# Three rearrangements of small TensorE work in a hybrid decoder layer: the adaLN columns, eight narrow transposes, and the bank of the state-space preparation

## The chip, the cores and the metric

The kernel runs on one core of a Trainium2 chip. The metric is the device time of one execution in microseconds.

## The reference

One decoder layer on 256 tokens of width 1024, all float32: a SwiGLU block (width 2816), then a mixing block (block-sparse attention with 8 heads beside a diagonal state-space layer with 32 groups, merged by sigmoid gates), then a second SwiGLU block, then a final norm. Each sub-layer's input is normalized, scaled and shifted, and its output is gated, by vectors that come from one conditioning vector c:

```python
ada = jax.nn.silu(c) @ w_ada[l] + b_ada[l]
sh1, sc1, g1, sh2, sc2, g2, sh3, sc3, g3 = jnp.split(ada, N_ADA, axis=-1)
h = modulate(rmsnorm(x, norm_ffn1[l]), sh1, sc1)
x = x + 0.5 * g1[:, None, :] * swiglu(h, w_ffn1_in[l], w_ffn1_out[l])
```

The nine vectors (numbers 0 to 8) have 1024 elements each. The kernel needs each as 128 partitions by 8 columns.

## The kernel before

Every weight comes from memory as float32, 1 MB at a time, into a ring of four buffers `raw`. ScalarE casts half of a buffer to `w_hi` (L296), VectorE makes the rest `w_lo` (L304), and each product is three matmuls (high by high, high by low, low by high): L327 to L329 for the tiles that go through `mm3`, L500 to L502 for the output projections, L649 for the first feed-forward's opening. One half buffer is a "quantum"; `state["q"]` counts them. A tile, or one step of an output projection, takes one quantum and is 24 matmuls with 256 columns.

Small TensorE work is put between the tiles by two means. `fill()` runs after most tiles and takes the first entry of the deque `pe_fill` if its due number has been reached. `pump()` moves the generator `ssm_prep` (the state-space preparation, 4 transposes of 128x128 at a time at L896, L910 and L935, and 64 small matmuls at L923) by one `yield`. A scheduler orders the traced instructions of every engine by what it takes to be ready, except inside `manual_schedule`; every engine then runs its list in that order, and a PSUM bank or a buffer that is taken anew waits for all readers and writers of its last use.

Vectors 0 and 1 are made at the start. The other seven are summed by VectorE over four weight blocks (`consume_ada`, L276) and handed to `ada_done`, which queues `do_cols` four quanta later. `do_cols` does all in one go, in one PSUM bank: eight passes with a matrix of ones add the partitions (L403), ScalarE copies the row sums to `ada_rows` (L408), two float32 products with four columns each (four passes, L410) turn them, and VectorE adds the bias (L390 to L395). The bank is `state["bank"]`: 3 in the first feed-forward and up to the four tiles that fill `U`, 1 in the 16 gate tiles and the branches behind them, 3 from the output projection on. The preparation uses banks 2 and 3.

The fills of the seven vectors, by the quantum at which they are due: vector 2 at 28, 4 at 42, 3 at 56 (first feed-forward), 5 at 84 (the last of the four `U` tiles), 7 at 92 and 6 at 100 (gate tiles; quanta 101 and 102 have no fill, 103 is the first branch tile), 8 at 162 (second feed-forward). `final_gain` (L1436) transposes the eight rows of `norm_final`, which a DMA puts in `rows[0]` (L1433), and is due at 148; the first fill of the second feed-forward is at 127. `rows[0]` held the vector c before that and was last read at the start (L1038).

Of the kernel before, what the change touches and what calls it, by code (L numbers as in the profile page):

```python
# [14 lines left out]
ALU = mybir.AluOpType  # L15
# [4 lines left out]
KD = D // 128  # L20
# [11 lines left out]
FILL_DELAY = 4  # L32
# [23 lines left out]
def kernel(ctx, tc, T, out):  # L56
    nc = tc.nc
# [33 lines left out]
    def bank(i):  # L91
        return psum.tile([128, 512], F32, tag=f"bank{i}", name=f"bank{i}")

    def sb(tag, shape, dt=F32, bufs=1, name=None):
        return parts[place.get(tag, "pool")].tile(shape, dt, tag=tag, name=name or tag, bufs=bufs)
# [129 lines left out]
    state = {"loaded": 0, "split": 0, "q": 0, "bank": 3}  # L225
# [4 lines left out]
    pe_fill = deque()  # L230
# [34 lines left out]
    def consume_ada(i):  # L265
        v, j = raw_items[i][3:]
        r = raw_tiles.pop(i)
        if j == 0:
            acc[v] = sb("acc", [128, D], bufs=2)
        a = acc[v]  # L270
        for k in range(2):
            cs = csil[:, 2 * j + k, 0:1]
            if j == 0 and k == 0:
                nc.vector.tensor_scalar(a, r[:, k, :], cs, None, op0=ALU.mult)
            else:
                nc.vector.scalar_tensor_tensor(out=a, in0=r[:, k, :], scalar=cs, in1=a, op0=ALU.mult, op1=ALU.add)  # L276
        if j == 3:
            ada_done(v)
# [53 lines left out]
    rows = [const.tile([n, 128], F32, name=f"rows{i}") for i, n in enumerate((8, 80, 56))]  # L332
# [23 lines left out]
    ident = const.tile([128, 128], F32, name="ident")  # L356
# [9 lines left out]
    bada = cols0[:, 0:72].rearrange("p (v k) -> p v k", k=KD)  # L366
    ldt = const.tile([128, 16], F32, name="ldt")
    norm_cols = {1: cols0[:, 72:80], 4: cols[:, 32:40], 7: cols[:, 40:48]}
# [15 lines left out]
    ada = {v: const.tile([128, KD], F32, name=f"ada{v}") for v in range(9)}  # L384

    def ada_cols(v, p, ks):

        o, b = ada[v][:, ks], bada[:, v, ks]
        if v in norm_cols:
            nc.vector.scalar_tensor_tensor(out=o, in0=p, scalar=1.0, in1=b, op0=ALU.add, op1=ALU.add)  # L390
            nc.vector.tensor_tensor(out=o, in0=o, in1=norm_cols[v][:, ks], op=ALU.mult)
        else:
            nc.vector.tensor_tensor(out=o, in0=p, in1=b, op=ALU.add)
            if v % 3 == 2:
                nc.vector.tensor_scalar(o, o, 0.5, None, op0=ALU.mult)  # L395

    def ada_done(v):
        a = acc.pop(v)

        def do_cols():  # L400
            p = bank(state["bank"])
            for q in range(4):
                nc.tensor.matmul(  # L403
                    p[32 * q:32 * q + 32, 0:256], ones[:, 0:32], a[:, q * 256:(q + 1) * 256], start=True, stop=True,
                    tile_position=(0, 32 * q),
                )
            rs = sb("ada_rows", [128, 256])
            nc.scalar.copy(rs, p[:, 0:256])  # L408
            for n in range(2):
                nc.tensor.matmul(  # L410
                    p[:, 256 + n:264:2], rs[:, n * 128:(n + 1) * 128], ident[:, ::32], start=True, stop=True
                )
            ada_cols(v, p[:, 256:264], slice(0, KD))

        pe_fill.append((state["q"] + FILL_DELAY, do_cols))

    block_sb = {}

# [14 lines left out]
    def ada_block_cols(b):  # L433
        a = block_sb.pop(b)
        p = bank(7)
        for n in range(2):
            nc.tensor.matmul(p[:, n:n + 1], a[:, n * 128:(n + 1) * 128], one1, start=True, stop=True)
        ks = slice(b, b + 1)
        ada_cols(1, p[:, 0:1], ks)
        ada_cols(0, p[:, 1:2], ks)  # L440
# [282 lines left out]
    def scratch(n):  # L723
        return [const.tile(P16, F32, name=f"scr{next(scr_n)}") for _ in range(n)]
# [107 lines left out]
    def ssm_prep():  # L832
# [10 lines left out]
        t, k, r, p = scratch(4)  # L843
# [45 lines left out]
        prep_ok[0] = False  # L889
        yield  # L890
        yield
        Cc = pcs[1]
        for i in range(2):
            p = bank(3)
            for j in range(4):
                nc.tensor.transpose(  # L896
                    p[:, j * 128:(j + 1) * 128], c_raw[i][:, j].rearrange("p a b -> p (a b)"), ident
                )
            pv = p.rearrange("p (i g c) -> p i g c", g=2, c=16)
            for g in range(2):  # L900
                rs = slice(64 * g, 64 * g + 64)
                for d in (Cc[i][rs], Cm[i][rs, :, g, :]):
                    nc.scalar.activation(d, pv[rs, :, g, :], AF.Copy, scale=-1.0 if i else 1.0)
            yield
        G = [sb(f"ssm_G{i}", [128, 16, 128]) for i in range(2)]
        for i in range(2):
            for q in range(4):
                p = bank(2 + q % 2)
                for n in range(4):
                    nc.tensor.transpose(  # L910
                        p[:, n * 128:(n + 1) * 128],
                        Gp[i][:, 4 * q + n].rearrange("p t g c -> p (t g c)"), ident,
                    )
                nc.scalar.copy(
                    G[i][:, 4 * q:4 * q + 4, :].rearrange("p a b -> p (a b)"), p
                )
                yield
        ssm["G"] = G
        p = bank(3)
        for j in range(4):  # L920
            for n in range(2):
                for q in range(4):
# [4 lines left out]
                        start=(n == 0), stop=(n == 1), tile_position=(0, 32 * q),  # L927
# [5 lines left out]
        p = bank(2)  # L933
# [10 lines left out]
        for t0 in range(4):  # L944
            rs = slice(32 * t0, 32 * t0 + 32)
# [81 lines left out]
    start = ExitStack()  # L1027
# [26 lines left out]
    for j in range(1, 4):  # L1054
# [19 lines left out]
        out=sel, in_=sel, compare_op=ALU.is_equal, fill=0.0, base=0, pattern=[[-1, 2], [0, 64]], channel_multiplier=1  # L1074
# [3 lines left out]
    for g in Gp + Cm + [ssm_L]:  # L1078
        nc.gpsimd.memset(g, 0.0)
    start.close()  # L1080
    prep = ssm_prep()

    def step1():
# [79 lines left out]
    for t in range(2):  # L1163
        nc.scalar.copy(vt[t], vb[t])

    U = sb("ssm_U", [128, 16, NC4 + 1])
    nc.gpsimd.memset(U[:, :, 0:1], 0.0)
    for j in range(4):
        p = bank(4 + j)[:, 0:S]
# [3 lines left out]
        for n in range(4):  # L1173
            for t in range(4):
                o = U[32 * t:32 * t + 32, 4 * j + n, 1:NC4 + 1]
                i_ = pv[32 * n:32 * n + 32, t, :]
# [7 lines left out]
    def s_mm(f):  # L1184
        S_b[f] = (bank(2), bank(3))
        for i in range(8):
            for n in range(2):
                nc.tensor.matmul(  # L1188
                    S_b[f][n][:, i * 64:(i + 1) * 64], ssm["G"][n][:, 8 * f + i, :],
                    U[:, 8 * f + i, 0:NC4], start=True, stop=True,  # L1190
                )
# [40 lines left out]
    def y_mm(f, m):  # L1232
# [5 lines left out]
        for y in range(3):  # L1238
            for n in range(4):
# [4 lines left out]
                else:  # L1244
                    st, mv = ssm["L"][:, ii, t, :], U[:, ii, 1:NC4 + 1]
                nc.tensor.matmul(  # L1246
# [96 lines left out]
    for hd in range(8):  # L1343
        n = 2 * hd - (hd > 6)
# [11 lines left out]
    for n in range(16):  # L1356
        g, j = divmod(n, 8)
        p = bank(4 + n % 3)[:, 0:S]
# [34 lines left out]
    for q in range(4):  # L1393
        p = bank(4 + q)
# [7 lines left out]
    for q in range(4):  # L1402
        p = bank(4 + q)
# [22 lines left out]
    ks = range(KD - HOLD, KD)  # L1426
# [11 lines left out]
        nc.tensor.transpose(p[:, 0:KD], rows[0], ident[0:8, 0:8])  # L1438
        nc.vector.tensor_copy(nf, p[:, 0:KD])

    pe_fill.append((state["q"] + 30, final_gain))

    def each(g):
        if g == 0:
# [37 lines left out]
    for t in range(2):  # L1482
        o = sb(("ssm_Pr", "ssm_Pi")[t], [128, D])
# [37 lines left out]
```

## Time and profile before

| | |
|---|---|
| median of 3 runs | 613.01 us (611.45 to 613.42) |
| the profiled execution | 611.65 us |
| its span, first to last instruction | 609.5 us |
| TensorE matmuls busy | 598.2 us (98%) x5328 |
| VectorE busy | 456.1 us (75%) |
| ScalarE busy | 326.9 us (54%) |
| mean granted TensorE clock | 0.988 |

A matmul's busy time is longer than the distance to the next one, since they are pipelined: 0.28 us each where a new one starts every 0.11 to 0.12 us. So the distance between starts is what to read, not the busy share. What lies outside the span is 2.1 us.

### The profile page before, as it was taken

Reading aid. Unit: us, or ns where it says so; the run is one execution under the profiler, and the core shown is the slowest. Engines: PE = TensorE matmul, PEld = TensorE weight load, DVE = VectorE, ACT = ScalarE, POOL = GpSimd, SP = SyncE. Lnnn points to the kernel's source line nnn. Section 1 sums busy time; section 2 is a strip of 40 time slices with the busy share of each in tenths; the row PEclk is TensorE's granted clock in tenths of the full one; section 3 lists DMA queues with packets and bytes.
Section 4 is the critical chain, followed back from the end, with each engine's and each line's share of the span. In section 5 each row is a group of like instructions: output and inputs, shape, how many; then the busy total and the mean of one; then the engine's idle time right before and its main releaser. Section 6 shows DMA issues by size and latency. Waiting matters only on the chain.

```text
span 609.5 us, 12820 instructions
## 1 busy us (share of the span) xinstructions
PE 598.2 (98%) x5328; PEld 571.3 (94%) x5328; DVE 456.1 (75%) x838; ACT 326.9 (54%) x537; POOL 25.3 (4%) x37
## 2 busy tenths in 40 slices
PE   7999999999999999999999999999999999999996
PEld 7888999999999999998987899999999999999995
DVE  2689999889867569998999859968975646445433
ACT  4445856469435445846536865447744444444434
POOL 6201010020000001000000000001000000000000
PEclk8999999999999999998999999999999999999997
DMA  9999989875969555888448836564586746745201
GB/s 278 335 312 247 362 276 368 280 263 177 317 212 343 178 172 172 312 270 284 139 140 282 276 135 208 195 221 139 208 275 209 247 168 233 249 149 200 70 2 70
DMA packets 97770, 136.70 MB, mean 224 GB/s; under 512 B 7761, under 2 KB 77474, under 8 KB 97712
## 3 DMA queue, kind: packets, MB, share of 16 engines
q1 hardware_dynamic: 97424, 135.81, 66.8%
q8 instruction: 42, 0.69, 0.5%
q14 instruction: 16, 0.13, 0.1%
q0 software_dynamic: 288, 0.07, 0.1%
HBM read 134.82 MB, written 1.05 MB: 223 GB/s over the span
## 4 chain that ended last, share of the span: by engine, by line
PE 88%; DVE 4%; DMA 4%; ACT 2%; issue 1%; POOL 0%; SPq 0%; ACTq 0%; DVEq 0%
PE bank L327 16%; PE bank L328 16%; PE bank L329 16%; PE bank L500 8%; PE bank L501 8%; PE bank L502 8%; PE bank L649 5%; DVE w_lo L304 2%; PE bank L425 1%; DMA raw<-in_w_in_dram 1%; PE bank L1246 1%; DMA raw<-in_w_ada_dram 1%; PE bank L1188 1%; DMA ssm_G<-in_w_ffn_in_dram 1%; DVE acc L276 1%
## 5 line engine op out<-in xcount | busy, mean ns | idle before, releaser
L304 DVE TENSOR_TENSOR w_lo<-raw,w_hi 128x1024 fp32r<-128x1024 f32 x168 | 204.2, 1223 | 84.2 <-ACT w_hi L296 83.8
L296 ACT CAST w_hi<-raw 128x1024 fp32r<-128x1024 f32 x168 | 174.0, 1048 | 165.5 <-PE bank L328 97.4
L327 PE MATMUL bank<-h_hi,w_hi 128*128 128x256 f32 x736 | 209.5, 285 | 0.0
L329 PE MATMUL bank<-h_hi,w_lo 128*128 128x256 f32 x736 | 207.1, 281 | 0.0
L328 PE MATMUL bank<-h_lo,w_hi 128*128 128x256 f32 x736 | 207.0, 281 | 0.0
L327 PEld LDWEIGHTS bank<-h_hi,w_hi 128*128 128x128 f32 x736 | 139.5, 190 | 3.9 <-issue 2.3
L329 PEld LDWEIGHTS bank<-h_hi,w_lo 128*128 128x128 f32 x736 | 140.0, 190 | 0.3 <-issue 0.2
L328 PEld LDWEIGHTS bank<-h_lo,w_hi 128*128 128x128 f32 x736 | 139.0, 189 | 0.1
L500 PE MATMUL bank<-a,w_hi 128*128 128x256 f32 x352 | 99.2, 282 | 0.0
L501 PE MATMUL bank<-a,w_hi 128*128 128x256 f32 x352 | 98.9, 281 | 0.0
L502 PE MATMUL bank<-a,w_lo 128*128 128x256 f32 x352 | 98.4, 280 | 0.0
L276 DVE SCALAR_TENSOR_TENSOR acc<-raw,csil,acc 128x1024 f32<-128x1024 f32 x49 | 62.8, 1281 | 7.8 <-DMA raw<-in_w_ada_dram 7.5
L500 PEld LDWEIGHTS bank<-a,w_hi 128*128 128x128 f32 x352 | 66.5, 189 | 1.0 <-issue 1.0
L502 PEld LDWEIGHTS bank<-a,w_lo 128*128 128x128 f32 x352 | 66.7, 190 | 0.0
L501 PEld LDWEIGHTS bank<-a,w_hi 128*128 128x128 f32 x352 | 66.1, 188 | 0.0
L327 PE MATMUL bank<-a,w_hi 128*128 128x258 f32 x112 | 31.9, 286 | 0.0
L328 PE MATMUL bank<-a,w_hi 128*128 128x258 f32 x112 | 31.8, 284 | 0.0
L329 PE MATMUL bank<-a,w_lo 128*128 128x258 f32 x112 | 31.5, 282 | 0.0
L649 PE MATMUL bank<-h_hi,w_hi 128*128 128x256 f32 x112 | 27.4, 294 | 0.9 <-ACT w_hi L296 0.5
L649 PE MATMUL bank<-h_lo,w_hi 128*128 128x256 f32 x112 | 27.8, 286 | 0.0
L649 PE MATMUL bank<-h_hi,w_lo 128*128 128x256 f32 x112 | 27.4, 283 | 0.0
L446 POOL TENSOR_TENSOR rstd<-rstd,mhalf 128x2 f32<-128x2 f32 x4 | 4.7, 1168 | 456.8 <-DVE rstd L445 456.8
(337 smaller groups left out, 893.0 us busy)
## 6 DMA issues: line engine op xcount, KB each, us to landing
raw<-in_w_ffn_in_dram SPq DMA_DIRECT2D x36, 1024.0 KB, 5.4
raw<-in_w_ada_dram SPq DMA_DIRECT2D x28, 1024.0 KB, 5.2
raw<-in_w_ffn_out_dram SPq DMA_DIRECT2D x22, 1024.0 KB, 5.3
raw<-in_w_in_dram SPq DMA_DIRECT2D x16, 1024.0 KB, 5.5
raw<-in_w_ada_dram SPq DMA_DIRECT2D x16, 512.0 KB, 8.1
raw<-in_w_out_dram SPq DMA_DIRECT2D x4, 1024.0 KB, 4.8
a<-in_w_ffn_in_dram SPq DMA_DIRECT2D x8, 448.0 KB, 7.1
ssm_G<-in_w_ffn_in_dram SPq DMA_DIRECT2D x4, 896.0 KB, 10.7
```

The source lines that it names most:

```text
L276: nc.vector.scalar_tensor_tensor(out=a, in0=r[:, k, :], scalar=cs, in1=a, op0=ALU.mult, op1=ALU.add)
L296: nc.scalar.copy(hi, r)
L304: nc.vector.tensor_tensor(out=lo, in0=r, in1=hi.bitcast(F32), op=ALU.subtract)
L327: nc.tensor.matmul(o, st[0], mv[0], start=first, stop=False)
L328: nc.tensor.matmul(o, st[0], mv[1], start=False, stop=False)
L329: nc.tensor.matmul(o, st[1], mv[0], start=False, stop=last)
L425: nc.tensor.matmul(p[q:q + 32, 0:256], csil[:, k, :], r[:, k, :], start=(k < 4), stop=(k >= 4), tile_position=(0, q))
L500: nc.tensor.matmul(mm3_o, wj[0], a[0], start=first and j % 2 == 0, stop=False)
L501: nc.tensor.matmul(mm3_o, wj[0], a[1], start=False, stop=False)
L502: nc.tensor.matmul(mm3_o, wj[1], a[0], start=False, stop=last and j % 2 == 1)
L649: nc.tensor.matmul(pb[b][:, n * S:(n + 1) * S], z[:, b * 128:(b + 1) * 128], h[hl][:, kb, :], start=(kb == 0 and n == 0 and y == 0), stop= ...
L1188: nc.tensor.matmul(S_b[f][n][:, i * 64:(i + 1) * 64], ssm["G"][n][:, 8 * f + i, :], U[:, 8 * f + i, 0:NC4], start=True, stop=True,)
```

## The change

`do_cols` becomes two entries of `pe_fill`. `sums` does the eight passes and the copy, and puts `turn_rows` at the head of the queue for the next quantum. `turn_rows` takes the bank anew, transposes the two halves of `ada_rows` whole (128x128, one pass each) and reads every 32nd column of the result; it then queues `spacer` for two quanta later. `spacer` takes the bank and transposes `rows[0]` (8 rows) into eight columns that nobody reads. One more `spacer` is queued ahead of the four `U` tiles. The preparation takes bank 2 for everything, and has one more `yield` before its first transposes. `final_gain` is due at 126 and no longer at 148.

```diff
     def ada_cols(v, p, ks):
-        o, b = ada[v][:, ks], bada[:, v, ks]
+        o, b, g = ada[v][:, ks], bada[:, v, ks], norm_cols[v][:, ks] if v in norm_cols else None
+        if len(p.shape) == 3:
+            o, b, g = (z if z is None else z.rearrange("p (q n) -> p q n", n=2) for z in (o, b, g))
...
+    def spacer():
+        p = bank(state["bank"])
+        nc.tensor.transpose(p[:, 0:8], rows[0], ident[0:8, 0:8])
+
     def ada_done(v):
         a = acc.pop(v)
-        def do_cols():
+        def sums():
             p = bank(state["bank"])
...
             rs = sb("ada_rows", [128, 256])
             nc.scalar.copy(rs, p[:, 0:256])
+            pe_fill.appendleft((state["q"] + 1, lambda: turn_rows(rs)))
+
+        def turn_rows(rs):
+            p = bank(state["bank"])
             for n in range(2):
-                nc.tensor.matmul(
-                    p[:, 256 + n:264:2], rs[:, n * 128:(n + 1) * 128], ident[:, ::32], start=True, stop=True
-                )
-            ada_cols(v, p[:, 256:264], slice(0, KD))
-        pe_fill.append((state["q"] + FILL_DELAY, do_cols))
+                nc.tensor.transpose(p[:, n * 128:n * 128 + 128], rs[:, n * 128:(n + 1) * 128], ident)
+            ada_cols(v, p[:, 0:256].rearrange("p (n q c) -> p q n c", n=2, q=4)[:, :, :, 0], slice(0, KD))
+            pe_fill.append((state["q"] + 2, spacer))
+        pe_fill.append((state["q"] + FILL_DELAY, sums))
...
         yield
         yield
+        yield
         Cc = pcs[1]
         for i in range(2):
-            p = bank(3)
+            p = bank(2)
...
-                p = bank(2 + q % 2)
+                p = bank(2)
...
-        p = bank(3)
+        p = bank(2)
...
+    pe_fill.appendleft((0, spacer))
     U = sb("ssm_U", [128, 16, NC4 + 1])
...
-    pe_fill.append((state["q"] + 30, final_gain))
+    pe_fill.append((state["q"] + 8, final_gain))
```

## Rows read from the trace of the kernel before

**Rows 1.** The page's 40 equal slices of the span: granted TensorE clock in tenths.
```profile
PEclk8999999999999999998999999999999999999997
```
**Rows 2.** Stretches of the span, busy us (x instructions) by engine.
```profile
core 0: us, PE busy (x) PEld busy (x) DVE busy (x) ACT busy (x) POOL busy (x), PEclk, DMA share, GB/s
...
155.00:192.00 37.00, 37.00 (x329) 37.00 (x327) 28.59 (x30) 15.44 (x17) 0.00 (x0) 1.00 0.80 275
195.00:230.00 35.00, 35.00 (x299) 35.00 (x298) 21.19 (x37) 15.38 (x22) 0.00 (x0) 1.00 0.55 180
...
360.00:410.00 50.00, 50.00 (x427) 50.00 (x426) 39.87 (x66) 25.02 (x37) 0.00 (x0) 1.00 0.59 197
439.00:496.00 57.00, 57.00 (x487) 57.00 (x486) 36.43 (x35) 24.51 (x28) 0.00 (x0) 1.00 0.69 233
497.00:534.50 37.50, 37.50 (x333) 37.50 (x332) 22.14 (x20) 16.71 (x19) 0.00 (x0) 1.00 0.68 225
537.00:592.00 55.00, 55.00 (x469) 55.00 (x468) 25.74 (x27) 20.98 (x23) 0.00 (x0) 1.00 0.32 109
```
**Rows 3.** Timeline, TensorE matmuls around the narrow transpose: start us, us, line, operation.
```profile
496.21 0.28 PE L329 MATMUL bank<-h_hi,w_lo 128*128 128x256 f32 x1
496.42 0.22 PE L1438 MATMUL bank<-ident,rows 8*128 8x8 f32 x1
496.57 0.38 PE L327 MATMUL bank<-h_hi,w_hi 128*128 128x256 f32 x1
496.80 0.28 PE L328 MATMUL bank<-h_lo,w_hi 128*128 128x256 f32 x1
```
**Rows 4.** Timeline, TensorE matmuls around vector 8's products with four columns.
```profile
536.24 0.28 PE L500 MATMUL bank<-a,w_hi 128*128 128x256 f32 x1
536.35 0.50 PE L410 MATMUL bank<-ident,ada_rows 128*128 128x4 f32 x4
...
536.92 0.28 PE L502 MATMUL bank<-a,w_lo 128*128 128x256 f32 x1
```
**Rows 5.** Timeline, TensorE matmuls around two wide transposes of the attention.
```profile
351.30 0.29 PE L328 MATMUL bank<-h_lo,w_hi 128*128 128x256 f32 x1
351.42 0.39 PE L1306 MATMUL bank<-ident,at_e 128*128 128x128 f32 x2
...
351.76 0.28 PE L327 MATMUL bank<-h_hi,w_hi 128*128 128x256 f32 x1
```
**Rows 6.** Timeline, TensorE: the preparation's transposes, a tile of 24 between two groups.
```profile
101.24 0.60 PE L910 MATMUL bank<-ident,big 128*128 128x128 f32 x4
...
104.51 0.60 PE L910 MATMUL bank<-ident,big 128*128 128x128 f32 x4
...
111.37 0.66 PE L910 MATMUL bank<-ident,big 128*128 128x128 f32 x4 [0.43 <-DVE ada L393]
112.79 0.60 PE L910 MATMUL bank<-ident,big 128*128 128x128 f32 x4
115.97 0.60 PE L910 MATMUL bank<-ident,big 128*128 128x128 f32 x4
```
**Rows 7.** Waits of TensorE's weight loads: us in total, times, longest.
```profile
PEld bank L410 <- ACT ada_rows L408: 1.2, 2, 1.0
```
**Rows 8.** Timeline around vector 5's copy and products.
```profile
276.38 0.37 ACT L408 COPY ada_rows<-bank 128x256 f32<-128x256 f32 x1
276.81 0.61 PE L410 MATMUL bank<-ident,ada_rows 128*128 128x4 f32 x4 [0.81 <-ACT ada_rows L408]
```
**Rows 9.** Two stretches there, columns as in rows 2.
```profile
274.30:277.70 3.40, 2.59 (x25) 2.02 (x25) 3.22 (x9) 3.17 (x11) 0.00 (x0) 1.00 1.07 371
277.70:281.10 3.40, 3.40 (x18) 3.40 (x18) 3.20 (x9) 1.86 (x5) 0.00 (x0) 0.51 0.99 353
```
**Rows 10.** Timeline, TensorE: the first four of vector 6's eight sum passes.
```profile
357.84 0.42 PE L403 MATMUL bank<-acc,ones 128*32 128x256 f32 x4
```
**Rows 11.** Instructions that touch `rows`: the final norm's DMA, its duration and issue.
```profile
L1433 SPq DMA_DIRECT2D rows<-in_norm_final_dram x1: 362/362/362, 115.6 to 115.6; - x1
```

More of the change, by code (lines that the diff above doesn't have):

```diff
@@ L386, in ada_cols @@
     def ada_cols(v, p, ks):
-        o, b = ada[v][:, ks], bada[:, v, ks]
+        o, b, g = ada[v][:, ks], bada[:, v, ks], norm_cols[v][:, ks] if v in norm_cols else None
+        if len(p.shape) == 3:
+            o, b, g = (z if z is None else z.rearrange("p (q n) -> p q n", n=2) for z in (o, b, g))
         if v in norm_cols:
             nc.vector.scalar_tensor_tensor(out=o, in0=p, scalar=1.0, in1=b, op0=ALU.add, op1=ALU.add)
-            nc.vector.tensor_tensor(out=o, in0=o, in1=norm_cols[v][:, ks], op=ALU.mult)
+            nc.vector.tensor_tensor(out=o, in0=o, in1=g, op=ALU.mult)
         else:
```

## The prediction

> **What bounds the kernel now.** I read the page first. TensorE works from end to end, and its clock is full in 37 of 40 slices; the exceptions are the first, the last and one near 280 us [rows 1]. So a microsecond is won only where TensorE's own stream of matmuls gets shorter: fewer passes, fewer waits, a lost clock given back, or a shorter distance between matmuls.
>
> The last of these is what I then looked at, by counting matmuls in stretches where nothing but 24-matmul tiles runs and TensorE is busy all the time [rows 2]. A row counts each matmul that is still running at the left edge: at 0.28 us each and one every 0.115 us that is 2.4 too many. From 155 to 192 us this gives 37.0 / (329 - 2.4) = 113.3 ns from one matmul to the next; from 497 to 534.5 us, 37.5 / 330.6 = 113.4 ns. But from 195 to 230 us it is 35.0 / 296.6 = 118.0 ns, from 360 to 410 us 117.8, from 439 to 496 us 117.6, and from 537 to 592 us 117.9. All six have the same clock (1.00), the same 256 columns and a full TensorE. So there are two step lengths, 4.4 ns or 3.7% apart, and a stretch keeps the one it has for hundreds of matmuls. The reader is to see that the level has nothing to do with how busy VectorE, ScalarE or the DMAs are: the 155 row has the highest DMA share (0.80), the 537 row the lowest (0.32).
>
> What changes the level lies at the borders of the stretches. 118 becomes 113 at 496.4 us, where the stream is broken by one thing only, the narrow transpose of `final_gain` [rows 3]. 113 becomes 118 at 536.4 us, at vector 8's four-column products [rows 4]; vector 3's, between the 155 and the 195 us row, do the same; vector 6's stand ahead of the 360 us row. Vector 4's, just ahead of 155 us, leave 113. So L410 goes to the long step three times in four. Why a level holds is not to be seen in any row; I use it as found.
>
> **The change part by part.** *Four-column products to wide transposes.* From the last matmul before L410 to the second after it are 536.92 - 536.24 = 0.68 us, and two ordinary steps would be 0.23, so a turn costs 0.45 us; seven cost 3.2 [rows 4]. Two wide 128x128 transposes of the attention: 351.76 - 351.30 = 0.46 us against the same 0.23, so 0.23 us; seven cost 1.6 [rows 5]. The preparation's groups of four bear that out: 115.97 - 112.79 = 3.18 us less 24 x 113.3 ns is 0.46 for four [rows 6]. Net -1.6 us. VectorE's strided read is of eight elements as before, and the row copy is the same.
>
> *The spacers.* From the matmul before the narrow transpose to the second after it: 496.80 - 496.21 = 0.59 us, less two steps of 0.118, is 0.35 us [rows 3]. There are eight new ones (seven vectors, one before `U`): +2.8 us. They lie in TensorE's stream and nothing hides them. Bounds: 0.15 us each if only the step 496.42 to 496.57 counted (1.2 us), and 0.35 plus a wait for the bank's last reader, of which the trace has one of 0.43 us [rows 6], so 6.2 us. I take 2.8, since two tiles (5.6 us) after its turn the bank has long been read.
>
> *Waits.* L410 waits for the copy that `do_cols` itself has just ordered: 1.2 us in two waits, the longer 1.0 us [rows 7], which is the one at 276.8 us [rows 8]. A tile later the copy is done, so the short one, 0.2 us, goes. One preparation group waits 0.43 us for VectorE to read vector 2's columns, because both use bank 3 [rows 6]; with the preparation in bank 2 that goes too. -0.6 us. In place of it each group of transposes now waits for the copy of the group before it, a whole tile earlier (3.2 us) [rows 6]; I take nothing, at most 0.4 us for each of ten groups. The preparation's extra `yield` shifts it by one tile and costs no instruction.
>
> *The wait at 276.8 us and the clock.* There TensorE stood idle 0.81 us ahead of L410 and was busy for 2.59 of 3.4 us; in the next 3.4 us the granted clock was 0.51, which is the lower level of 1.2 GHz nearly throughout, with 18 matmuls instead of some 30 [rows 8, 9]. That is (18 - 2) x (213 - 113 ns) = 1.6 us lost, 213 ns being 3.4 us / 16. Together 2.6 us with the whole 1.0 of the wait. The turn now comes a tile later and in bank 1. But behind the sums in bank 3 come the state-space products that need bank 3 as well, and they need the same copy L408 to be over, so they can inherit the wait. Both ends are open, 0 and -2.6; I take half, -1.3.
>
> *The step length.* This is the large term. A spacer is the same instruction as L1438, on the same eight rows, so I take it to leave the short step as that did. By the due numbers in the code and a tile of 2.83 us, the stretches that now run long behind one are: vector 3's spacer at quantum 59, three after its sums at 192 us where the 155 us row ends, so 201 to 230 us, 29 us; vector 6's at 105, five after the sums at 357.84 us [rows 10], so 372 to 412, 40 us; `final_gain`, now at quantum 127 and 21 tiles ahead of 496.4, so 437 to 496, 59 us; vector 8's at 165, three after its sums at about 535 us, ahead of rows 4, so 543 to 592, 49 us. Together 177 us x 3.7% = 6.6 us, and three `U` tiles of 24 matmuls x 4.4 ns = 0.3. Total -6.9 us. Vectors 2, 5 and 7 lie among small work that breaks the stream every tile: nothing either way. Vector 4's stretch is short already.
>
> The bounds are 0 (no flip) and -6.9. There is one clean instance of the flip, L1438, so this is the term to doubt. The wide transposes speak less clearly: of the preparation's groups, the one at 112.79 is followed by a short tile (3.18 us to the next) and the one at 101.24 by a longer one (104.51 - 101.24 = 3.27 us, 24 x 4 ns more) [rows 6]. That is why I rest on the spacer and leave the two tiles between turn and spacer out of the sum.
>
> **Sum.** -1.6 + 2.8 - 0.6 - 1.3 - 6.9 = -7.6 us on the profiled execution's 611.65 us (span 609.5 and 2.1 around it): 604.05 us. The runs shown lie at 611.45 to 613.42 with a median 1.36 us above the profiled one; I add half of that, 0.7, and forecast 604.7 us.
>
> **The rivals.** *No flip.* The level is set by something that only coincides with L1438, such as the phase of a wait or where the weights lie. Then the term of 6.9 is 0 and the sum is -0.7: 611.65 us once the same 0.7 is added, 611 to 613. For it: there is one instance only. Against it: at 496.4 us no wait, no clock step and no change of stage stands beside the transpose [rows 3]. Chance 0.13. The Trainium skill speaks for this rival: "TensorE: Matmul & The Clock Gate", section "Back-to-back issue gap", gives the distance between warm matmuls by their columns alone, 262 cycles or about 109 ns for 256. By that rule no transpose could shorten the tiles behind it; the trace does not agree that there is a single value, since it has 113 and 118 ns at one clock.
>
> *Half of it.* The level is drawn anew at each spacer and half of the four long stretches get the short one: 604.7 + 3.4 = 608.1 us. For it: the groups of L910 draw both. Chance 0.18.
>
> *Slower: the short stretches are lost.* If the wide pair and the spacer leave the long step, the 155 and 497 us rows go to it too: (37 + 37.5) x 3.9% = 2.9 us, on top of no flip elsewhere. That is 611.65 + 2.9 = 614.6 us, and 615.9 if the clock term gives nothing either. In this last case it decides from 1.9 us on, or 49 us of lost short stretch. For it: L410 does just this, and the tile after 101.24 is long. Against it: L1438. Chance 0.09.
>
> *A late DMA.* `norm_final` was loaded at 115.6 us [rows 11], since `rows[0]` was free; now every spacer up to quantum 105 reads `rows[0]`, so its issue waits on SP until about 372 us, with the weight loads of the output projection queued behind it. If the issue stands one tile too early in SP's order, loads come 2.8 us late, and the ring of four buffers (two quanta each) covers most of that. At most 2.8 us, 607.5; `final_gain` itself has 65 us after it. Chance 0.04.
>
> **How the numbers follow.** The forecast has 0.56 and its own range is 601.8 to 607.5: down by the other half of the clock term (1.3) and the cheaper spacers (1.6), up by one stretch of the four not flipped (1.7) and a few spacers' waits. The range of 8 in 10 reaches down to 600.3, where the two tiles ahead of the four spacers are short too (0.8) and the 0.7 is not to be added, and up to 611.5 over the cases of half (0.18), the late DMA (0.04) and the lower part of no flip. Faster by over 0.3%, about what a measurement of this kernel can tell from no change (under 611.2), takes the first, the half, the DMA and a little of no flip: 0.79; within 0.3% (to 614.9): 0.13; slower: 0.08.
>
> **What would show it.** Right: the matmul count of 35, 50, 57 and 55 us as in rows 2 rises by about 3.8% behind the new spacers, L910 shows no wait for VectorE, L1438 stands near 437 us. Wrong: those counts stay at one per 118 ns; or a spacer shows an idle time before it; or the clock falls to 0.5 in a slice where it is now full. If the state-space products wait for L408 near 276 us and the clock dips again, only the half credit of 1.3 was wrong.

## The result, and the profile after

Changed kernel: 605.08 us median of 4 runs (603.43 to 605.20). Kernel before, on the same chip: 612.23 us median of 4 (610.46 to 613.42). Ratio 0.9884, 95% interval 0.9856 to 0.9911: faster by 0.9% to 1.4%. The profiled execution took 604.96 us, 6.69 us less than that of before; the sum had said 7.6 less.

The granted clock in 40 slices of the span: the slice near 280 us that stood at 8 in [rows 1] is at 9 here.
```profile
PEclk9999999999999999999999999999999999999997
```
The stretches that answer to [rows 2], with two more: 64 to 91 us, which had 230 matmuls before, and the 3.5 us around vector 5's sums and row copy.
```profile
core 0: us, PE busy (x) PEld busy (x) DVE busy (x) ACT busy (x) POOL busy (x), PEclk, DMA share, GB/s
64.00:91.00 27.00, 27.00 (x238) 26.92 (x237) 27.00 (x44) 18.18 (x33) 2.11 (x1) 1.00 0.87 311
155.00:192.00 37.00, 37.00 (x327) 36.85 (x325) 30.42 (x35) 15.44 (x17) 0.00 (x0) 1.00 0.80 274
195.00:230.00 35.00, 35.00 (x307) 34.85 (x306) 22.31 (x40) 16.75 (x24) 0.00 (x0) 1.00 0.50 164
360.00:410.00 50.00, 50.00 (x440) 49.85 (x439) 40.81 (x68) 25.61 (x38) 0.00 (x0) 1.00 0.57 192
439.00:496.00 57.00, 57.00 (x506) 57.00 (x505) 35.37 (x34) 25.66 (x28) 0.00 (x0) 1.00 0.72 240
537.00:592.00 55.00, 55.00 (x480) 54.47 (x479) 26.88 (x29) 23.19 (x30) 0.00 (x0) 1.00 0.29 97
272.00:275.50 3.50, 2.62 (x25) 1.94 (x24) 3.13 (x9) 3.06 (x7) 0.00 (x0) 1.00 1.05 375
```
Read the x of TensorE: 299 became 307, 427 became 440, 487 became 506 and 469 became 480. The 57 us row holds nothing but tiles: 57.0 / (506 - 2.4) = 113.2 ns where it had 117.6. All the stretches that were long are short now, which is what the prediction wanted to see. But whether the *spacers* did this is a question for the border, not for the count. TensorE's timeline from vector 6's wide turn (L421) to its spacer (L402):
```profile
366.00 0.28 PE L329 MATMUL bank<-ssm_Pr,w_lo 128*128 128x256 f32 x1
366.11 0.38 PE L421 MATMUL bank<-ident,ada_rows 128*128 128x128 f32 x2
366.25 0.37 PE L328 MATMUL bank<-ssm_Pi,w_hi 128*128 128x256 f32 x1
366.45 0.28 PE L329 MATMUL bank<-ssm_Pr,w_lo 128*128 128x256 f32 x1
...
371.56 0.28 PE L329 MATMUL bank<-ssm_Pr,w_lo 128*128 128x256 f32 x1
371.77 0.22 PE L402 MATMUL bank<-ident,rows 8*128 8x8 f32 x1
```
From 366.45 to 371.56 us lie 45 steps of ordinary matmuls: 5.11 / 45 = 113.6 ns. The stream was short *before* the spacer came. The same reading ahead of the spacers at 201.36 and 539.36 us gives 113 ns too. At these three places the spacer had nothing to shorten. Ahead of vector 2's, at 118.38 us, the stream was short as well. The one before `U`, at 264.41 us, did meet a long stream and leave a short one (117.8 ns before, 113.6 after).

TensorE's waits, total, times, longest, in us; the first two were foreseen as 0 to 0.4 and as an open question, the third not at all:
```profile
PE bank L921 <- ACT v L914: 1.5, 1, 1.5
PE bank L1200 <- ACT ada_rows L415: 1.1, 1, 1.1
PE bank L329 <- DVE w_lo L304: 0.7, 1, 0.7
```
The first is the preparation in one bank: its second set of transposes (L921) waits at 101.23 us until ScalarE has copied the set before it. The second is the wait of [rows 7, 8], handed on from the turn to the state-space products behind it:
```profile
275.24 0.37 ACT L415 COPY ada_rows<-bank 128x256 f32<-128x256 f32 x1
275.67 2.00 PE L1200 MATMUL bank<-ssm_U,ssm_G 128*128 128x64 f32 x16 [1.05 <-ACT ada_rows L415]
```
The late DMA did no harm: its issue stands at 372.0 us as worked out, and `final_gain` at 434.6 us had no idle time before it, though TensorE's sequencer for weight loads had waited 2.06 us ahead of it; what for, the trace doesn't name.
```profile
L1445 SPq DMA_DIRECT2D rows<-in_norm_final_dram x1: 300/300/300, 372.0 to 372.0; - x1
L1450 PEldq EVENT_SEMAPHORE  x1: 2061/2061/2061, 432.4 to 432.4; - x1
```

### The profile page after: what moved, and what is told of

Read it like the earlier page. It is cut to its first block, busy times and chain, and to the rows that moved or that the text cites. A ratio compares the mean times of both kernels' runs of the same rounds, so it can differ in the third digit from the quotient of the medians.

```text
span 602.9 us, 12799 instructions
## 1 busy us (share of the span) xinstructions
PE 588.3 (98%) x5322; PEld 559.5 (93%) x5322; DVE 455.8 (76%) x838; ACT 326.7 (54%) x537; POOL 25.1 (4%) x37
## 4 chain that ended last, share of the span: by engine, by line
PE 83%; DMA 6%; DVE 5%; ACT 3%; issue 1%; SPq 0%; POOLq 0%; DVEq 0%; ACTq 0%
PE bank L327 16%; PE bank L328 16%; PE bank L329 16%; PE bank L510 8%; PE bank L511 8%; PE bank L512 8%; PE bank L659 4%; DMA raw<-in_w_ffn_in_dram 2%; DMA raw<-in_w_in_dram 1%; DMA a<-in_w_ffn_in_dram 1%; DMA raw<-in_w_ada_dram 1%; PE bank L435 1%; ACT w_hi L296 1%; DVE w_lo L304 1%; PE bank L1200 1%
## 5 line engine op out<-in xcount | busy, mean ns | idle before, releaser
L327 PE MATMUL bank<-h_hi,w_hi 128*128 128x256 f32 x736 | 206.6, 281 | 0.0
L329 PE MATMUL bank<-h_hi,w_lo 128*128 128x256 f32 x736 | 204.6, 278 | 0.7 <-DVE w_lo L304 0.7
L328 PE MATMUL bank<-h_lo,w_hi 128*128 128x256 f32 x736 | 204.2, 278 | 0.0
L329 PEld LDWEIGHTS bank<-h_hi,w_lo 128*128 128x128 f32 x736 | 138.3, 188 | 1.7 <-DVE w_lo L304 0.8
L510 PE MATMUL bank<-a,w_hi 128*128 128x256 f32 x352 | 98.4, 280 | 0.0
L511 PE MATMUL bank<-a,w_hi 128*128 128x256 f32 x352 | 97.7, 277 | 0.0
L659 PE MATMUL bank<-h_hi,w_hi 128*128 128x256 f32 x112 | 27.3, 293 | 1.4 <-ACT h_hi L487 0.9
L659 PE MATMUL bank<-h_lo,w_hi 128*128 128x256 f32 x112 | 27.7, 285 | 0.1
L659 PE MATMUL bank<-h_hi,w_lo 128*128 128x256 f32 x112 | 27.2, 282 | 0.0
```

Source lines behind the costliest of these rows:

```text
L327: nc.tensor.matmul(o, st[0], mv[0], start=first, stop=False)
L328: nc.tensor.matmul(o, st[0], mv[1], start=False, stop=False)
L329: nc.tensor.matmul(o, st[1], mv[0], start=False, stop=last)
L510: nc.tensor.matmul(mm3_o, wj[0], a[0], start=first and j % 2 == 0, stop=False)
L511: nc.tensor.matmul(mm3_o, wj[0], a[1], start=False, stop=False)
L659: nc.tensor.matmul(pb[b][:, n * S:(n + 1) * S], z[:, b * 128:(b + 1) * 128], h[hl][:, kb, :], start=(kb == 0 and n == 0 and y == 0), stop= ...
```

## The experiments

Theory A, the prediction's: a narrow transpose leaves the short step, so the spacers shorten the stretches behind them. Theory B: the four-column products make the stream long, so taking them away is what counts, and spacers only cost. Theory C: the level is drawn at each border, and the changed kernel was lucky.

Each ratio is to runs of the kernel before on the same chip (medians 611.68, 611.54, 611.45 and 611.73 us on the four chips).

Some sums below come from *matched* profiles. The kernel before, the changed one and those of e0 to e8 all run the same 4400 matmuls of 256 or 258 columns (the tiles, the output projections and the vectors made at the start), in the same order except among the branches, from about 310 to 367 us. So the n-th of one profile can be set beside the n-th of another, and where the distance between the two grows, time was lost there.

### e0, the kernel before once more

> The kernel before, once more, for the step lengths alone. If a level belongs to the program, the matmul counts from 155 to 192, 195 to 230, 360 to 410, 439 to 496 and 537 to 592 us come out as 329, 299, 427, 487 and 469 again, within 3. If a level is drawn anew in each execution, at least one of them moves by 8 or more, to the other level.

One run, 610.66 us. Two stretches changed places with the profile of before, 155 to 192 us (329 there) and 195 to 230 us (299 there):
```profile
155.00:192.00 37.00, 37.00 (x317) 37.00 (x316) 28.65 (x31) 15.49 (x17) 0.00 (x0) 1.00 0.90 310
195.00:230.00 35.00, 35.00 (x310) 35.00 (x309) 22.27 (x39) 15.88 (x24) 0.00 (x0) 1.00 0.54 176
```
Its waits of TensorE have vector 5's products again:
```profile
PE bank L410 <- ACT ada_rows L408: 1.1, 1, 1.1
```
The other stretches were as in [rows 2]. So the level behind a turn is not fixed by the program: here vector 4's products left long and vector 3's short, the other way round than before. The wait of 1.1 us was there as well, but no slice of the clock row fell. So the 1.6 us of lost clock, half of which the prediction booked as a gain, come and go between executions of one kernel.

### e1, `final_gain` early and nothing else

```diff
-    pe_fill.append((state["q"] + 30, final_gain))
+    pe_fill.append((state["q"] + 8, final_gain))
```


> The kernel before with one edit: final_gain is due 8 quanta after its queueing and not 30. Spacer theory (a narrow transpose leaves the short step of 113 ns): the narrow transpose stands near 437 us, the 57 us from 439 to 496 us hold some 505 matmuls instead of 487, nothing else moves, and the time falls by 2.2 us (ratio 0.996). Chance theory (every break draws a level): 505 or 487, as likely the one as the other. Cost theory (the transpose only takes its 0.35 us): 487 matmuls, ratio 1.000.

608.25 us (607.81 to 609.29), ratio 0.9944 [0.9927, 0.9962]: 3.4 us, where 59 us of short step are worth 2.2. The two profiled executions are 2.4 us apart (609.29 and 611.65). In e1's, 64 to 91 us ran short too (238 matmuls for 230, 8 x 0.113 = 0.9 us), with the same program there as before, and other places took that back. So the last 1 us or so of the 3.4 is not this edit's as far as a profile shows.
```profile
439.00:496.00 57.00, 57.00 (x506) 57.00 (x504) 36.83 (x37) 26.00 (x30) 0.00 (x0) 1.00 0.71 236
```
Moving one narrow transpose forward moved the border with it, from 496 to 437 us. This one edit of the change does what the prediction said of it. In all eleven profiles (before, after, e0 to e8) `final_gain` met a long stream and left a short one.

### e2, the spacers alone

The kernel before with `spacer` defined as in the change, and one line more at the end of `do_cols`; none ahead of `U`.
```diff
             ada_cols(v, p[:, 256:264], slice(0, KD))
+            pe_fill.append((state["q"] + 2, spacer))
```


> The kernel before with a spacer two quanta after each vector's columns; the four-column products, both banks of the preparation and final_gain stay as they were. Spacer theory: the four-column products leave the long step and the spacer ends it two tiles later, so counts of about 307, 440 and 480 from 195 to 230, 360 to 410 and 537 to 592 us, 487 still from 439 to 496; gain 4.4 us less seven times 0.35, about -1.9 us (ratio 0.997). Wide-turn theory (the four-column products are what lengthens the step, and their removal is the gain): counts as before, +2.5 us (ratio 1.004).

612.34 us (611.03 to 614.80, 10 runs), ratio 1.0011 [0.9995, 1.0026]. No gain.
```profile
195.00:230.00 35.00, 35.00 (x299) 34.31 (x299) 20.48 (x34) 15.94 (x22) 0.00 (x0) 1.00 0.58 182
360.00:410.00 50.00, 50.00 (x441) 48.99 (x440) 39.56 (x64) 25.95 (x41) 0.00 (x0) 1.00 0.62 200
537.00:592.00 55.00, 55.00 (x470) 54.31 (x469) 27.44 (x29) 22.80 (x26) 0.00 (x0) 1.00 0.35 116
```
Of three long stretches with a spacer near their start, one (360 us) went short and two did not (299 and 470, as before). Theory A falls here: the same instruction, on the same rows, in the same kind of stream, left long at 202.1 and at 544.6 us. A spacer that meets a short stream leaves it short: so at 162.3 us here, and at six more places in the changed kernel's two profiles.

### e3 and e7, the changed kernel without its spacers

```diff
-            pe_fill.append((state["q"] + 2, spacer))
...
-    pe_fill.appendleft((0, spacer))
```


> The changed kernel without its eight spacers; wide turns, the preparation's bank and the early final_gain stay. Wide-turn theory: the step stays short after the turns, counts as in the changed kernel (307, 440, 506, 480 in the four stretches), and eight times 0.35 us is saved: about 602 us, ratio to the kernel before 0.984. Spacer theory: a wide pair leaves either level, so one or two of the three stretches behind a turn (35, 50 and 55 us) go back to the long step, 1.3 to 1.9 us each, and the time is 603.5 to 605.5 us, ratio 0.987 to 0.990; the 57 us behind final_gain stay at 506.

603.18 us (602.17 to 603.53), ratio 0.9861 [0.9845, 0.9878].
```profile
195.00:230.00 35.00, 35.00 (x308) 35.00 (x308) 22.86 (x40) 17.63 (x25) 0.00 (x0) 1.00 0.50 159
360.00:410.00 50.00, 50.00 (x441) 50.00 (x441) 42.64 (x70) 28.05 (x41) 0.00 (x0) 1.00 0.59 190
537.00:592.00 55.00, 55.00 (x483) 54.61 (x482) 26.54 (x30) 23.91 (x33) 0.00 (x0) 1.00 0.26 85
```
All short with no spacer in the kernel. It ran again (e7) beside the changed kernel (e6), to see whether the spacers cost anything that can be measured.

> e3's kernel again. If wide pairs keep the short step in every execution, all runs lie within 602 to 603.6 us and the counts of its profile are those of e3 within 3 (308, 441, 505, 483). If its four short stretches were a lucky draw, at least one goes back to 118 ns (a count lower by 9 or more) in this profile, and the runs reach 605 us.

> The changed kernel again, beside e3's kernel on one chip. If the spacers only cost their passes it is 1.9 to 2.8 us above e7: 605 us, ratio 0.9885. If they hold the level where a draw would lose it in other executions, e7 scatters upward by 1.3 us and more and the two meet.

e7: 603.66 us (602.30 to 607.20), ratio 0.9873 [0.9832, 0.9914], counts again short everywhere. e6: 604.07 us (603.49 to 607.29), ratio 0.9882 [0.9845, 0.9919]. The changed kernel is 0.4 us slower there, and by the ratios of e3 and of the result 0.0023, or 1.4 us; the intervals overlap. The medians show no gain from the spacers and don't settle their cost. Matched, the changed kernel's first profile loses 0.35 us to e3's at each of the spacers behind vectors 4, 3, 6 and 8, which is their passes and no more.

One of e7's four runs took 607.20 us. By the expectation for e7, a run at 605 us speaks for a draw, and no trace of that run was kept. So the short stretches of e3's kernel are shown for the profiled executions and not for every execution.

e6's profiled execution, the slowest of its four at 607.29 us, shows both pieces failing. Its timeline of TensorE from vector 4's wide turn to the spacer:
```profile
155.98 0.44 PE L421 MATMUL bank<-ident,ada_rows 128*128 128x128 f32 x2
...
156.37 0.28 PE L328 MATMUL bank<-h_lo,w_hi 128*128 128x256 f32 x1
...
158.49 0.28 PE L328 MATMUL bank<-h_lo,w_hi 128*128 128x256 f32 x1
...
162.55 0.22 PE L402 MATMUL bank<-ident,rows 8*128 8x8 f32 x1 [0.48 <-DVE ada L392]
```
Behind the turn 18 steps take 2.12 us, 117.8 ns: a wide turn can leave long too, here one that took 0.44 us where the others took 0.38. The spacer, which stood idle 0.48 us for the turn's columns, did not shorten the stream; nor did the next one, at 203.46 us, which had no wait. So 155 to 192 and 195 to 230 us held 308 and 297 matmuls where 327 and 307 had been.

### e4, four-column products put back

The kernel of e3 with the old products in `turn_rows`, so still one tile behind the sums, with `final_gain` early and one bank for the preparation.
```diff
             for n in range(2):
-                nc.tensor.transpose(p[:, n * 128:n * 128 + 128], rs[:, n * 128:(n + 1) * 128], ident)
-            ada_cols(v, p[:, 0:256].rearrange("p (n q c) -> p q n c", n=2, q=4)[:, :, :, 0], slice(0, KD))
+                nc.tensor.matmul(
+                    p[:, 256 + n:264:2], rs[:, n * 128:(n + 1) * 128], ident[:, ::32], start=True, stop=True
+                )
+            ada_cols(v, p[:, 256:264], slice(0, KD))
```


> The kernel of e3 (no spacers) with the four-column products in place of the wide transposes, still one tile after the sums: only the shape of the turn differs. Shape theory (four-column products lengthen the step, wide pairs leave it short): two or three of the stretches behind vectors 4, 3, 6 and 8 go to 118 ns, 1.3 to 2.1 us each, and each of seven turns costs 0.2 us more: 606 to 608.5 us, ratio to the kernel before 0.992 to 0.996. Delay theory (a turn that waits for nothing leaves the step as it was, whatever its shape): all stay short, only the 1.6 us for the passes, about 604.7 us, ratio 0.988.

613.26 us (610.38 to 615.04, 10 runs), ratio 1.0026 [1.0002, 1.0050]: the whole gain gone, and with 10 us to e3 more than expected.
```profile
155.00:192.00 37.00, 37.00 (x316) 37.00 (x316) 29.45 (x34) 15.48 (x17) 0.00 (x0) 1.00 0.80 282
195.00:230.00 35.00, 35.00 (x299) 35.00 (x298) 21.33 (x37) 15.28 (x22) 0.00 (x0) 1.00 0.51 166
360.00:410.00 50.00, 50.00 (x426) 48.75 (x426) 38.97 (x62) 25.79 (x42) 0.00 (x0) 1.00 0.60 198
497.00:534.50 37.50, 37.50 (x333) 37.50 (x332) 21.59 (x21) 17.26 (x19) 0.00 (x0) 1.00 0.66 224
537.00:592.00 55.00, 55.00 (x470) 55.00 (x469) 26.90 (x27) 21.68 (x25) 0.00 (x0) 1.00 0.34 115
```
Long behind all four, vector 4's too. The two kernels differ in these products alone. At vectors 4, 6 and 8 the stream was short (113.3 ns) up to the products and long (117.8) behind them; ahead of vector 8 the row from 497 us shows it. At vector 3 it was long already and stayed so. The two profiles are 10.4 us apart. Matched, the four stretches give 5.5 of that; the products' own price is 7 x (0.455 - 0.232) = 1.6 (p2 and p3, below), the wait of the state-space products for `ada_rows` is 0.9 longer (1.2 for 0.3), and the clock near 280 us fell, 1.6. The last two came and went between other profiles of one kernel too, so the 10 us are not the products' alone.

### e5, wide transposes at once

The kernel of e3 with the wide transposes right behind the row copy, in the other half of the same bank: no delay, no spacers.
```diff
             nc.scalar.copy(rs, p[:, 0:256])
-            pe_fill.appendleft((state["q"] + 1, lambda: turn_rows(rs)))
-
-        def turn_rows(rs):
-            p = bank(state["bank"])
             for n in range(2):
-                nc.tensor.transpose(p[:, n * 128:n * 128 + 128], rs[:, n * 128:(n + 1) * 128], ident)
...
+                nc.tensor.transpose(
+                    p[:, 256 + n * 128:384 + n * 128], rs[:, n * 128:(n + 1) * 128], ident
+                )
```


> The kernel of e3 with the wide transposes right behind the row copy, as do_cols had it, and not a tile later: only the delay differs. Shape theory: the stretches behind vectors 4, 3, 6 and 8 stay short, about 603 us plus up to 1 us where the turn waits for the copy, ratio 0.986 to 0.988. Delay theory: two or three of them go to 118 ns, 605 to 608 us, ratio 0.990 to 0.994.

602.71 us (601.56 to 603.61), ratio 0.9848 [0.9818, 0.9877]; every stretch short (329, 309, 441, 505 and 483 matmuls). The delay of one tile is not needed for the step, and without it the wait near 276 us is the turn's own again (the first row here; e3's state-space products had waited 0.3 us there):
```profile
PE bank L417 <- ACT ada_rows L415: 1.1, 1, 1.1
PE bank L918 <- ACT v L911: 0.8, 1, 0.8
```
The delay has a price elsewhere, among the branches. Between the same two tile matmuls lie 57.4 us in the kernel before and 59.5 in the changed one, first and last row of each:
```profile
296.65 0.28 PE L328 MATMUL bank<-h_lo,w_hi 128*128 128x256 f32 x1
...
354.05 0.28 PE L329 MATMUL bank<-h_hi,w_lo 128*128 128x256 f32 x1
```
```profile
293.86 0.28 PE L328 MATMUL bank<-h_lo,w_hi 128*128 128x256 f32 x1
...
353.33 0.28 PE L329 MATMUL bank<-h_hi,w_lo 128*128 128x256 f32 x1
```
In e5 and e8 they are 57.0 and 57.1 us, in all five profiles with the delay (the changed kernel, e3, e4, e6, e7) 59.2 to 59.5, a spacer's 0.35 us included where there is one. TensorE's work is the same there but for vector 7's turn and that spacer; its order is another, and the 0.7 us wait for `w_lo` lies there, which only those five profiles have.

### e8, the first transposes of the preparation back in bank 3

```diff
         for i in range(2):
-            p = bank(2)
+            p = bank(3)
```
On e5, for the 0.8 us of its second row.

> e5's kernel with the preparation's first two groups of transposes back in bank 3, so that the next groups, in bank 2, don't wait for ScalarE's eight copies out of the same bank. TensorE's order is the same, only a bank differs. If the wait of 0.8 us that e5 shows there is the price of the single bank, it is gone and the time is some 0.8 us lower, 602 us (ratio to the kernel before 0.984). If it is ScalarE's lateness alone, whatever the bank, the wait stays. The step lengths stay short behind vectors 4, 3, 6 and 8 (329, 309, 441, 483).

602.17 us (601.14 to 603.65), ratio 0.9846 [0.9816, 0.9876]. The wait for L911 is gone from the list, as it should be if the one bank made it. One profile doesn't prove that: with one bank the wait stood in four profiles (the changed kernel, e4, e5, e6: 0.7 to 1.5 us) and not in e3 and e7, the two that ran long from 64 to 91 us and so came to that place 0.9 us later. e8 ran short there (237 matmuls) and had no wait, which speaks for the bank. The time is the same as e5's within the intervals. By the medians either is below the changed kernel by about 2 us, with less code than it; the intervals overlap.

### p1 to p3, one kind of transpose after each step of the second feed-forward

One run each; the body of `probe()` was a narrow transpose (p1), two wide ones (p2) or two four-column products (p3), on `ident`, into a bank that nobody reads.
```diff
+    def probe():
+        if pe_fill and pe_fill[0][0] <= state["q"]:
+            fill()
+            return
+        p = bank(3)
+        nc.tensor.transpose(p[:, 0:8], ident[0:8, :], ident[0:8, 0:8])
...
-    r = ffn(h, ada[8], 0, fill, lambda: each, raw=raw2, final=True)
+    r = ffn(h, ada[8], 0, probe, lambda: each, raw=raw2, final=True)
```


> The kernel before, with one narrow transpose (8 rows of the identity into bank 3, never read) after each of some 50 steps of the second feed-forward. It measures what the step length is behind a narrow transpose: spacer theory 113 ns behind at least 95% of them; chance theory some mixture, with the share as the number sought. Each costs 0.35 us before any gain of step length.

> The same with two wide 128x128 transposes after each step. Shape theory: 113 ns behind nearly all. Chance theory: a mixture, as behind the preparation's groups of four (before: 8 short, 1 long). Each pair costs 0.23 us.

> The same with two float32 products of four columns after each step. Shape theory: 118 ns behind most of them (three of four in the trace of before), so that the tiles from 439 to 592 us are long nearly throughout. Chance theory: the same mixture as behind the other two forms. Each pair costs 0.45 us.

630.64, 622.93 and 630.80 us, with 611.73 for the kernel before. TensorE's timeline of p1, then p2, then p3, the probes alone:
```profile
438.32 0.22 PE L1486 MATMUL bank<-ident 8*128 8x8 f32 x1
...
441.42 0.22 PE L1486 MATMUL bank<-ident 8*128 8x8 f32 x1
...
444.59 0.22 PE L1486 MATMUL bank<-ident 8*128 8x8 f32 x1
...
447.69 0.22 PE L1486 MATMUL bank<-ident 8*128 8x8 f32 x1
...
450.87 0.22 PE L1486 MATMUL bank<-ident 8*128 8x8 f32 x1
```
```profile
441.25 0.38 PE L1487 MATMUL bank<-ident 128*128 128x128 f32 x2
...
444.23 0.38 PE L1487 MATMUL bank<-ident 128*128 128x128 f32 x2
...
447.20 0.38 PE L1487 MATMUL bank<-ident 128*128 128x128 f32 x2
```
```profile
438.87 0.50 PE L1487 MATMUL bank<-ident 128*128 128x4 f32 x4
...
442.06 0.50 PE L1487 MATMUL bank<-ident 128*128 128x4 f32 x4
...
445.24 0.50 PE L1487 MATMUL bank<-ident 128*128 128x4 f32 x4
```
The narrow ones stand 3.10, 3.17, 3.10 and 3.18 us apart in turn: 24 steps of 113.3 ns are 2.72 us and of 117.8 ns 2.83, so the tiles between them are short, long, short, long, 27 to 26 in all. A narrow transpose in this rhythm goes to the *other* level: not always to the short one, and not as if drawn either. The wide ones left the short step 52 times in 53, and the four-column products, in this rhythm, 53 times in 53, though the same shape left long behind all four vectors of e4. p3's products differ from e4's in more than the rhythm: they read `ident`, and nobody reads what they make. The prices, from the last matmul before to the second after less two steps, as medians: 0.352 us for a narrow one, 0.232 for a wide pair, 0.455 for a four-column pair. Times 53 these are 18.7 us for p1, which took 18.9 more than before; 24.1 for p3, which took 19.1, less because it also made some 110 us of long stretches short (about 4 us); and 12.3 for p2, which took 11.2 where the same 4 us should have left 8.3. p2's profile also lost the clock near 280 us and ran long behind vector 4 (317 matmuls from 155 to 192 us), and 0.9 us more than usual of its time lies outside the span (622.93 less 619.9 us). These may be the difference; one run each doesn't settle it.

## Why the prediction was right, and where not

The time was right (604.7 for 605.08). The large term's size was about right too, and its reason was wrong, so that its size came out is luck in part.

**The step that failed** is "A spacer is the same instruction as L1438, on the same eight rows, so I take it to leave the short step as that did". In e2 spacers left long two times in three, in p1 they alternate, and at three of the four places in the changed kernel the stream was short before they came. What shortened 201 to 230, 372 to 412 and 543 to 592 us (4.4 of the 6.6 us) is the removal of the four-column products: e3 and e5 keep it without a spacer, e4 gives it back with nothing else changed. Counted over the five profiles with these products (before, e0, e1, e2, e4), the stream was long right behind 16 of 20 turns of vectors 4, 3, 6 and 8; over the six with wide turns, behind 2 of 24, both in e6, and one of those two was long before its turn. The remaining 2.2 us came from `final_gain` moved forward, shown alone by e1. The prediction had the right row in hand, "L410 goes to the long step three times in four", and used it only to say where the spacers have something to repair, not what happens when L410 is gone. Its remark that the wide transposes "speak less clearly" kept it from seeing that a wide pair in the place of L410, at these four vectors, leaves a short stream short (22 times in 23).

**The rivals.** *No flip* fell: all four stretches changed. *Half of it* had the truer mechanism, a draw at each border, but not the size, since behind the wide turns the clean stretches came out short in all but one profile. *Slower* did not come about in the first profiled execution; in e6's its mechanism was there, with two short stretches lost behind a wide turn and its spacer, and 607.29 us. *A late DMA* came at the time worked out, and no cost of it shows. The page of the Trainium skill named in the prediction, "TensorE: Matmul & The Clock Gate", section "Back-to-back issue gap", calls the 262 cycles for 256 columns the gap of an isolated matmul; for a stream in which each matmul has its weight load, as here, it says that both operations set the spacing, which the prediction left out. It lists one figure for each number of columns either way, and 113 and 118 ns at one granted clock in e4 and e5, with the same tiles, do not agree with that.

**The terms**, on the two profiled executions:

| term | predicted, us | seen, us | from |
|---|---|---|---|
| turns | -1.6 | -1.6 | 7 x (0.455 - 0.232), p2 and p3 |
| spacers | +2.8 | +2.8 | 8 x 0.352, p1; 0.35 each, matched with e3; 0.4 to 1.4 by medians |
| waits gone | -0.6 | -0.6 | [rows 6, 7]; neither is in the list of after |
| one bank for the preparation | 0 | +1.5 | L921's wait |
| `U` wait and clock | -1.3 | -1.5 | clock -1.6, and 1.0 of wait became 1.1 |
| step, four stretches and `U` | -6.9 | -6.5 | matched: 0.95 + 1.4 + 2.2 + 1.6, and 0.3 at `U` |
| step, tiles ahead of those spacers | 0 | -0.9 | matched: 0.2 + 0.5 + 0.2 at vectors 3, 6 and 8 |
| step, 64 to 91 us | none | -0.9 | 238 for 230 |
| order among the branches | none | +1.9 | 59.5 - 57.4, less spacer and turn; 0.7 of it is the wait for `w_lo` |
| sum | -7.6 | -5.8 | measured -6.7 |

The bound of 0.4 us for the one-bank wait was wrong: it looked at the four groups that stand a tile apart in [rows 6] and not at two sets of transposes that come behind one another. That the clock term came out near the half that the sum had booked is chance, since e0 kept its clock with the old code. The 0.9 us at 64 us belongs to no part of the change; e1 drew it too, e3 did not. The 1.9 us among the branches is the largest cost that the prediction had at nothing: it gave the later turn a gain in waits, and no price for the order that it changes. The 0.9 us that the seen terms leave of the measured 6.7 lie in small pieces (0.3 ahead of 64 us, 0.2 behind 586 us, the rest about the borders), and were not traced to a cause.

**What each part is worth.** Wide turns and the early `final_gain` make the gain. The tile of delay gives nothing for the step and costs about 2 us among the branches (e5), of which e5 loses 0.8 again in the wait near 276 us. Behind vectors 4, 3, 6 and 8 the spacers shorten nothing in either profile of the changed kernel, and they cost 0.35 us each (the changed kernel matched with e3). The one bank costs a wait in four profiles of six; with bank 3 back (e8) it is gone.

**What stays open.** Theory C is right in part: which level a border leaves is drawn anew between executions of one kernel (e0, e6), and by the same shape differently in different places (e4, p3). At vector 5, among the attention's products, it is even the other way round: the delayed wide pair left 48 matmuls at 117.8 ns in all four profiles that have it, and e4's four-column products left them at 113.3. So the shape alone doesn't make the level; what is shown is what each turn did at vectors 4, 3, 6 and 8. There the changed kernel was not merely lucky: without the four-column products and without spacers the stretches were short in every profile of e3, e5, e7 and e8, one profile of each. No row shows what the level hangs on, nor why it then holds for hundreds of matmuls.

## What to carry to other kernels

In a stream that is TensorE from end to end, count matmuls per stretch: two step lengths 4% apart can be worth more than all the passes in dispute (here 6.5 us of step against 2.8 us of spacers), and the small work at a stretch's border decides between them. One instance of a flip is no rule; before leaning on it, look at what stands at the *other* border, where the bad level begins, for taking that away needs no repair. When a change has several parts, run it without each.

## What was not expected of the hardware

- The step of a matmul with 256 columns has two levels, 113.3 and 117.8 ns, at a granted clock of 1.00, and keeps one until small work breaks the stream. A single narrow transpose per tile makes it alternate (p1), while single ones in a short stream left it short seven times in seven (the changed kernel twice, e2).
- A pair of four-column float32 products costs 0.455 us in the stream (p3), nearly twice the 0.232 of a pair of 128x128 transposes (p2), though it has 16 columns in place of 256; one transpose of 8 rows costs 0.352 (p1), more than two full ones.
- In the changed kernel TensorE's sequencer for weight loads waited 2.06 us from 432.4 us on, ahead of `final_gain`, and no idle time of the engine is recorded there.
